# A whole-model kernel whose GpSimd makes part of the weights' low halves: another share for GpSimd, an earlier search, an earlier start of the gating

## Chip, cores and metric

The kernel runs on one core of a Trainium2 chip. The metric is the device time of one execution in microseconds (us), the lower the better. Engines are PE (TensorE, with PEld for its weight loads), DVE (VectorE), ACT (ScalarE), POOL (GpSimd) and SP (SyncE, which issues the DMAs of the weights).

## What is computed

Two transformer-like blocks on 256 tokens of 1024 features, all in float32. The first block is attention beside a gated recurrence, then PEER, a layer of 16384 experts of one neuron each, of which a token takes 16 for each of 8 heads. The second block is a convolution beside a linear recurrence (RG-LRU) with a gated linear layer behind it, and then a stick-breaking attention with another one. The change lies around PEER:

```python
def peer(x, wq, subkeys, u, v):                  # of one block of tokens xb
    qp = (xb @ wq).reshape(..., PEER_HEADS, 2, PEER_DKEY // 2)
    s = jnp.einsum('thcd,hcnd->thcn', qp, subkeys)      # 2 x 8 rows of 128 scores a token
    v1, i1 = lax.top_k(s[:, :, 0], 16)
    v2, i2 = lax.top_k(s[:, :, 1], 16)
    cand = v1[..., :, None] + v2[..., None, :]
    sc, p = lax.top_k(cand.reshape(..., 256), 16)       # eidx = (i1, i2) at p
    gates = jax.nn.softmax(sc, axis=-1)
    act = jax.nn.gelu(jnp.einsum('td,thkd->thk', xb, u[eidx]))
    return jnp.einsum('thk,thkd->td', gates * act, v[eidx])
```

## The kernel before

**Weights.** All weights stream through `load` in units of [128, 2048], two halves each. SyncE issues the DMA into `raw` (two buffers), ScalarE rounds a half to `hi` (L163), and `lo = raw - hi` (L168) is made by VectorE or by GpSimd; three buffers each of `hi` and `lo`, one unit ahead of use. A product takes three matmuls: x's high and low part by `hi`, and x's high part by `lo`. In `wstat` they make one chunk of 128 output columns with sixteen matmuls by `hi` (L196, L197) and then eight by `lo` (L199). So TensorE comes to a chunk's `lo` only after its sixteen matmuls by `hi`.

**Who makes `lo`.** `self.nsplit` counts the halves. GpSimd takes two of three halves of `pu` in its first 22 units and every other one behind them, and three of the first four halves of `wq`, `wi0`, `fgu0`, `wi1`, `fgu1`, the weights which follow a norm: 86 of 500 in all. VectorE makes the other 414.

**PEER.** Its stages are the query projection `wq` (16 chunks, each with two matmuls by `sk` that give the scores `s`, copied from PSUM for four columns at a time, L692), `pu` (128 chunks, every expert for all tokens, with GELU into `actA` and `actB`), and `pv` (the sum back over all experts). The gates of experts that a token doesn't take are zero. `topk` is the search of the sixteen best on VectorE. `best` takes two rounds of MAX8 and FIND_INDEX8 with one MATCH_REPLACE8 between (L719 to L722), over 128 scores or 64 sums. The sums `cand` (L735), the places, and the one-hots `oh` (L771 to L773) that look the places up follow. The search of the first 128 tokens (t = 0) and then that of the others are spread over the chunks of `pu` below `JT` = 56. From chunk 56 on `gate4` turns the places of four tokens into gates: one-hots A (L794) and B (L795) on VectorE, four matmuls of 128x128 (L797), products into the cells (L800, L803), and a copy by ScalarE of the chunks to come (L805). There are 64 of them, at chunks 56 to 123. `ga` (L818) is the product of the new chunk's GELU with the gates there already.

**Order.** The program is written in one sequence, and a scheduler gives each engine its own order; the queues run in order. The norms (`norm_t`) are chains of steps of one element a partition on VectorE (L291, L292 in `rsqrt1`); the first weights of the next product are split beside them. In `even`, ScalarE runs the tanh, exp and square root of the recurrence (L1024 to L1035) between the `hi` casts of `wi0`; the change of function costs an ACT_TABLE_LOAD.

Of the kernel before, what the change touches and what calls it, by code (L numbers as in the profile page):

```python
# [88 lines left out]
def layout(i):  # L89
# [11 lines left out]
    u = g("peer_u")[0].reshape(128, 64, 2, 8, 128)          # i1, unit, i2, k, p  # L101
# [32 lines left out]
# ---------------------------------------------------------------- the program  # L134
class Prog:
# [3 lines left out]
    # ---- streamed weights: units of [128, 2048], two halves each with hi and lo parts  # L139
    def stream_init(self):  # L140
# [7 lines left out]
        self.nsplit = 0  # L148

    LA = 1  # L150
    FIRST = ("wq", "wi0", "fgu0", "wi1", "fgu1")

    def load(self, n):
# [5 lines left out]
        for h in range(2):  # L159
# [21 lines left out]
    # ---- products  # L181
# [6 lines left out]
    def wstat(self, half, x, K=8):  # L188
        """W^T x for one chunk of 128 columns -> PSUM [128, 256]"""
# [12 lines left out]
    def xstat(self, acc, half, x, k, first, last, cg, ts=(0, 1)):  # L202
        """acc[t][c] += x_k^T W_k; x: hi, lo of [128, k, 256], or of [128, 128] for each t; cg: 512-column slices"""
# [16 lines left out]
    def out_n(self, nm, x, nk, step=None):  # L220
        """x^T W (K = nk*128, 1024 columns) -> acc[t][c] in PSUM; the first tokens are done first"""
# [17 lines left out]
    def out_n512(self, nm, j0, x, lead=0, step=None):  # L239
        """x^T W (K = 1024, 512 columns) -> acc[t] in PSUM; the first tokens lead by so many k"""  # L240
# [41 lines left out]
    def rsqrt1(self, pool, x):  # L282
        """x ** -0.5 for x [128, 1]"""
# [22 lines left out]
    def norm_t(self, pool, side, gain, shift=None, row=None):  # L306
        """rmsnorm(h) * gain (+ shift), hi and lo, features on partitions; gain, shift [128, 8];
        with a row, h is first replaced by rmsnorm(h) * row"""
# [89 lines left out]
    # ---- first block: MoBA attention and HGRN2  # L398
    def mix1(self):
# [20 lines left out]
        # f = lb + (1 - lb) (1 + tanh(x/2)) / 2  # L420
# [6 lines left out]
        # forget gates, queries  # L427
# [17 lines left out]
        for hd in range(4):  # L445
# [25 lines left out]
        # decayed products by halving: scT[b] holds s on partitions, (head, t) free  # L471
# [52 lines left out]
        def soft(c, qT, kT):  # L524
            """probabilities of heads 2c, 2c+1"""
# [26 lines left out]
                # (k0,q0) (k0,q1) (k1,q1)  # L552
# [13 lines left out]
        def decay(n=1):  # L566
            """n more levels begun, and those begun before done"""
# [74 lines left out]
    def add_res(self, t):  # L642
        """h += what the last stage left in PSUM, for tokens t"""
# [16 lines left out]
    # ---- PEER  # L660
    JT = 56

    def peer(self):
# [7 lines left out]
        with tc.tile_pool(name="pe", bufs=1) as p:  # L671
# [22 lines left out]
            for c in range(16):  # L694
                if c % 2 == 0:
                    u = self.unit("wq", c // 2)
                pt = self.wstat(u[c % 2], x)
                qps[c] = p3.tile([128, 256], F32, name="qp", bufs=3)
                nc.scalar.copy(qps[c], pt)
                if c:  # L700
                    scores(c - 1)
            scores(15)
            skp.__exit__(None, None, None)

            # the sixteen best of each half, of their sums, and their gates
            def topk(t):
                v = p2.tile([128, 16, 16], F32, name="v")
                iu = p2.tile([128, 16, 16], U32, name="iu")
                vi = p2.tile([128, 16, 16], F32, name="vi")
                gv = p2.tile([128, 8, 16], F32, name="gv")  # L710
                gp = p2.tile([128, 8, 16], U32, name="gp")
                ab = [p2.tile([128, 8, 16], F32, name=f"ab{n}") for n in range(2)]
                ai = p2.tile([128, 8, 16], U32, name="ai")
                res = [p2.tile([128, 8, 16], F32, name=f"res{n}") for n in range(3)]
                sm = p2.tile([128, 8], F32, name="gsm")

                def best(src, val, idx):
                    for r in range(2):
                        nc.vector.max(out=val[:, 8 * r:8 * r + 8], in_=src)  # L719
                        nc.vector.max_index(out=idx[:, 8 * r:8 * r + 8], in_max=val[:, 8 * r:8 * r + 8], in_values=src)  # L720
                        if r == 0:
                            nc.vector.match_replace(out=src, in_to_replace=val[:, 0:8], in_values=src, imm_value=-3.0e38)  # L722
# [21 lines left out]
                nc.vector.tensor_tensor(res[2], gv, gv[:, :, 0:1].to_broadcast([128, 8, 16]), op=ALU.subtract)  # L744
# [4 lines left out]
                # places in the halves: a = max(0, p / 8 - 1, p / 4 - 6, p - 48), and b = p less where row a begins,  # L749
                # min(16 a, 8 a + 8, 4 a + 24, a + 48)  # L750
# [471 lines left out]
```

## Time and profile before

| | |
|---|---|
| time, median of 3 runs | 1726.06 us (1725.60 to 1726.34) |
| span of the profiled execution | 1725.1 us |
| PE busy | 1606.9 us (93%) |
| DVE busy | 1320.7 us (77%) |
| ACT busy | 848.9 us (49%) |
| POOL busy | 251.2 us (15%), of which `lo` 213.7 us in 86 instructions |

The busy time of PE is an average over stages. The stages of PEER by the start of their first matmul: the query projection from 172.5 us, `pu`'s chunks 0 to 55 from 227.3, its chunks 56 to 127 from 415.5, `pv` from 706.2 to 1040. Columns of a timeline row: start, duration, engine, line, operation, output<-inputs, shape, count, and in brackets the idle time of the engine before it and what ended that. PE rows of a line are grouped where they follow each other (x8 is one chunk's eight matmuls by `lo`).

### The profile page before, as it was taken

To read this page: it belongs to the slowest core of one execution; us is meant where nothing else is said; L and a number is where in the kernel's file an instruction comes from. 1 tells how busy PE (TensorE), PEld (TensorE's weight loads), DVE (VectorE), ACT (ScalarE), POOL (GpSimd) and SP (SyncE) were. 2 spreads that over 40 slices of the span, in tenths; PEclk is the share of its full clock that TensorE was granted. 3 is DMA by queue.
4 is the path that set the end of the run, shared out by engine and by line. 5 is a ranking of instruction groups with operands and counts; after the bars stand their busy time and mean duration, and the time that the engine had idled before them with its cause. 6 is when DMAs were issued, how large, how long until landed. Compare 5 with 4: busy or idle time off the path is not lost.

```text
span 1725.1 us, 27616 instructions
## 1 busy us (share of the span) xinstructions
PE 1606.9 (93%) x10454; PEld 1461.7 (85%) x10454; DVE 1320.7 (77%) x2862; ACT 848.9 (49%) x1501; POOL 251.2 (15%) x113
## 2 busy tenths in 40 slices
PE   6997997899999998999999996997999799979998
PEld 6786997899999998888888885987998677769997
DVE  6967589834999999777787778877887778665544
ACT  6544452444433333555555554645444367754442
POOL 0302044443322233000000003001000100010000
PEclk9999998999999999999999998998999999989999
DMA  5424543364433343677777774564988643325554
GB/s 199 139 87 141 171 148 130 118 208 157 147 123 123 123 139 131 241 271 265 263 278 264 277 267 156 182 214 158 332 315 307 212 153 107 113 88 182 184 183 146
DMA packets 52405, 320.98 MB, mean 186 GB/s; under 512 B 5808, under 2 KB 6192, under 8 KB 20144
## 3 DMA queue, kind: packets, MB, share of 16 engines
q1 hardware_dynamic: 51264, 315.75, 52.6%
q10 hardware_dynamic: 1008, 3.47, 0.6%
q8 instruction: 82, 1.34, 0.3%
q14 instruction: 51, 0.42, 0.1%
HBM read 318.15 MB, written 1.05 MB: 185 GB/s over the span
## 4 chain that ended last, share of the span: by engine, by line
PE 70%; DVE 22%; issue 3%; ACT 3%; DMA 1%; POOL 0%; ACTq 0%; DVEq 0%; SPq 0%
PE acc L213 12%; PE acc L214 12%; PE acc L215 12%; PE pt L196 10%; PE pt L197 10%; PE pt L199 10%; DVE B L795 4%; DVE lo L168 3%; DVE A L794 3%; ACT hi L163 2%; DVE actA L800 1%; DVE oh L771 1%; PE pt L493 1%; DVE xn L302 1%; DVE actB L818 1%
## 5 line engine op out<-in xcount | busy, mean ns | idle before, releaser
L163 ACT CAST hi<-raw 128x1024 fp32r<-128x1024 f32 x500 | 524.2, 1051 | 483.7 <-PE pt L197 186.2
L168 DVE TENSOR_TENSOR lo<-raw,hi 128x1024 fp32r<-128x1024 f32 x414 | 513.4, 1241 | 294.9 <-ACT hi L163 289.7
L196 PE MATMUL pt<-xh,hi 128*128 128x256 f32 x2144 | 542.4, 290 | 11.9 <-ACT xh L357 11.2
L197 PE MATMUL pt<-xl,hi 128*128 128x256 f32 x2144 | 534.5, 286 | 0.4 <-DVE xl L358 0.4
L196 PEld LDWEIGHTS pt<-xh,hi 128*128 128x128 f32 x2144 | 417.8, 195 | 14.4 <-ACT xh L357 12.5
L197 PEld LDWEIGHTS pt<-xl,hi 128*128 128x128 f32 x2144 | 417.9, 195 | 0.9 <-DVE xl L358 0.7
L168 POOL TENSOR_TENSOR lo<-raw,hi 128x1024 fp32r<-128x1024 f32 x86 | 213.7, 2493 | 1137.9 <-ACT hi L163 858.4
L199 PE MATMUL pt<-xh,lo 128*128 128x256 f32 x2144 | 307.9, 287 | 17.2 <-DVE lo L168 17.2
L199 PEld LDWEIGHTS pt<-xh,lo 128*128 128x128 f32 x2144 | 282.2, 196 | 18.3 <-DVE lo L168 18.3
L214 PE MATMUL acc<-lo,wh 128*128 128x512 f32 x512 | 199.3, 389 | 0.7 <-DVE lo L168 0.7
L215 PE MATMUL acc<-hi,wl 128*128 128x512 f32 x512 | 199.3, 389 | 0.0
L213 PE MATMUL acc<-hi,wh 128*128 128x512 f32 x512 | 199.2, 389 | 0.0
L795 DVE TENSOR_SCALAR B<-iota,idxT,idxT 128x128 f32<-128x128 f32 x256 | 143.3, 560 | 0.0
L909 DVE SCALAR_TENSOR_TENSOR araw<-araw,sc 128x1024 f32<-128x1024 f32 x96 | 116.1, 1218 | 0.0
L214 PEld LDWEIGHTS acc<-lo,wh 128*128 128x128 f32 x512 | 96.1, 188 | 21.1 <-DVE lo L168 1.1
L215 PEld LDWEIGHTS acc<-hi,wl 128*128 128x128 f32 x512 | 96.1, 188 | 20.2 <-DVE wl L261 0.3
L213 PEld LDWEIGHTS acc<-hi,wh 128*128 128x128 f32 x512 | 96.1, 188 | 19.8
L805 ACT COPY actB<-acc 128x288 f32<-128x288 f32 (+31 forms) x64 | 18.4, 288 | 171.7 <-DVE actB L803 146.9
L797 PE MATMUL acc<-B,A 128*128 128x128 f32 x512 | 73.7, 280 | 17.7 <-DVE B L795 17.7
L794 DVE TENSOR_SCALAR A<-iota,idxT 128x128 f32<-128x128 f32 x256 | 88.4, 345 | 1.7 <-PE acc L797 1.7
L797 PEld LDWEIGHTS acc<-B,A 128*128 128x128 f32 x512 | 64.9, 192 | 21.9 <-DVE B L795 21.9
L214 PE MATMUL acc<-lo,yh 128*128 128x512 f32 x208 | 81.5, 392 | 0.0
(296 smaller groups left out, 1904.8 us busy)
## 6 DMA issues: line engine op xcount, KB each, us to landing
raw<-in_pu SPq DMA_DIRECT2D x64, 1024.0 KB, 4.9
raw<-in_pv SPq DMA_DIRECT2D x64, 1024.0 KB, 4.9
araw<-in_ada SPq DMA_DIRECT2D x96, 512.0 KB, 5.7
raw<-in_fgu SPq DMA_DIRECT2D x44, 1024.0 KB, 4.9
raw<-in_wi SPq DMA_DIRECT2D x22, 1024.0 KB, 4.9
raw<-in_fd SPq DMA_DIRECT2D x22, 1024.0 KB, 4.9
raw<-in_wp SPq DMA_DIRECT2D x14, 1024.0 KB, 5.0
raw<-in_wo SPq DMA_DIRECT2D x12, 1024.0 KB, 4.9
```

Of the source, the lines that this page charges most:

```text
L163: nc.scalar.copy(hi, s)
L168: ins = eng.tensor_tensor(lo, s, hi.bitcast(F32), op=ALU.subtract)
L196: nc.tensor.matmul(pt, hi[:, c], xh[:, k], start=k == 0, stop=False)
L197: nc.tensor.matmul(pt, hi[:, c], xl[:, k], start=False, stop=False)
L199: nc.tensor.matmul(pt, lo[:, k * 128:k * 128 + 128], xh[:, k], start=False, stop=k == K - 1)
L213: nc.tensor.matmul(a, xh, hi[:, cs], start=first, stop=False)
L214: nc.tensor.matmul(a, xh, lo[:, cs], start=False, stop=False)
L215: nc.tensor.matmul(a, xl, hi[:, cs], start=False, stop=last)
L794: nc.vector.tensor_scalar(A, iota, idxT[0][:, t:t + 1], None, op0=ALU.is_equal)
L795: nc.vector.tensor_scalar(B, iota, idxT[1][:, t:t + 1], idxT[2][:, t:t + 1], op0=ALU.is_equal, op1=ALU.mult)
L797: nc.tensor.matmul(gp[:, n], A, B, start=True, stop=True)
L909: nc.vector.scalar_tensor_tensor(w, w, 1.0, self.sc, op0=ALU.mult, op1=ALU.mult, accum_out=m[:, k:k + 1])
```

## The change

- GpSimd's share of `lo` is a table, `POOLED`: halves of `wq`'s units 2 to 7 and of `pu`'s units 0 to 5, so 24 halves, which are consecutive in the stream. VectorE makes the other 476. There is no GpSimd `lo` beside a norm or beside the gating.
- The search is cut in three. `halves` (the bests of the scores, both token halves in turn) starts at chunk 5 of the query projection; `sums` (the bests of the sums) and `places` come for t = 0 and t = 1 by a table of due chunks, `due`: fifteen steps in the chunks 0 to 11 of `pu`, fourteen in 12 to 33.
- `JT` is 40: the gating begins at chunk 40, and its 64 `gate4` lie in the chunks 40 to 123.
- Two small things of the second block go from GpSimd to VectorE: the scaling of `h` by the first norm (L361) and the two steps of `silu_c` in `even` (L883, L884).
- Comments are gone, so lines shift (L168 is L166 after; L719 to L722 are L700 to L703; A and B, L811 and L812; `ga`, L835; the recurrence of `even`, L1038 to L1049).

```diff
-    FIRST = ("wq", "wi0", "fgu0", "wi1", "fgu1")
+    POOLED = {"wq": (2, 8), "pu": (0, 6)}
...
-            self.nsplit += 1
-            eng = nc.vector
-            if (nm == "pu" and self.nsplit % (3 if j < self.JT // 2 - 6 else 2)) or (j < 2 and nm in self.FIRST and (j, h) != (1, 1)):
-                eng = nc.gpsimd
+            a, b = self.POOLED.get(nm, (0, 0))
+            eng = nc.gpsimd if a <= j < b else nc.vector
...
-                    nc.gpsimd.tensor_scalar(ht, ht, r1, None, op0=ALU.mult)
+                    nc.vector.tensor_scalar(ht, ht, r1, None, op0=ALU.mult)
...
-    JT = 56
+    JT = 40
...
+            def halves():
                 for c in range(16):
-                    best(s[t][:, c], v[:, c], iu[:, c])
-                    if c % 2 == 1:
-                        yield
+                    for t in range(2):
+                        best(s[t][:, c], v[t][:, c], iu[t][:, c])
+                    yield
+
+            def sums(t):
+                cand = p2.tile([128, 8, 64], F32, name="cand", bufs=2)
...
+                yield
                 for hd in range(8):
-                    best(cand[:, hd], gv[:, hd], gp[:, hd])
-                    yield
+                    best(cand[:, hd], gv[t][:, hd], gp[t][:, hd])
+                    if hd % 2:
+                        yield
+
+            def places(t):
...
+            hst = halves()
+            for c in range(16):
...
+                if c:
+                    scores(c - 1)
+                if c > 4:
+                    next(hst)
...
+            def steps():
+                yield from hst
+                for t in range(2):
+                    yield from sums(t)
+                for t in range(2):
+                    yield from places(t)
...
-            nst = 2 * (8 + 8 + 1 + 4 + 1)
-            k = 0
+            due = [i * 12 // 15 for i in range(15)] + [12 + i * 23 // 14 for i in range(14)]
+            n = 0
             for j in range(JT // 2):
                 u = self.unit("pu", j)
                 for h in range(2):
                     experts(2 * j + h, u[h])
-                while k < min(nst, (j + 1) * nst // (JT // 2 - 2) + 1):
-                    next(st, None)
-                    k += 1
+                    while n < len(due) and due[n] <= 2 * j + h:
+                        next(st, None)
+                        n += 1
...
-        self.silu_c(pa, self.sc, nc.gpsimd, 4)
+        self.silu_c(pa, self.sc, nc.vector, 4)
```

VectorE in the middle of the gating, before: the gates A and B of four tokens, the products (L800, L803, L818) and no `lo` in this chunk, which GpSimd makes.

```order
L818 TENSOR_TENSOR actB<-actB,ga 128x124
L800 TENSOR_TENSOR actA<-actA,acc 128x56x4
L803 TENSOR_TENSOR actB<-actB,acc 128x33x4
L794 TENSOR_SCALAR A<-iota,idxT_1689 128x128
L795 TENSOR_SCALAR B<-iota,idxT_1690,idxT_1691 128x128
L794 TENSOR_SCALAR A<-iota,idxT_1689 128x128
L795 TENSOR_SCALAR B<-iota,idxT_1690,idxT_1691 128x128
L794 TENSOR_SCALAR A<-iota,idxT_1689 128x128
L795 TENSOR_SCALAR B<-iota,idxT_1690,idxT_1691 128x128
L794 TENSOR_SCALAR A<-iota,idxT_1689 128x128
L795 TENSOR_SCALAR B<-iota,idxT_1690,idxT_1691 128x128
```

The same place after.

```order
L835 TENSOR_TENSOR actB<-actB,ga 128x124
L817 TENSOR_TENSOR actA<-actA,acc 128x40x4
L820 TENSOR_TENSOR actB<-actB,acc 128x41x4
L811 TENSOR_SCALAR A<-iota,idxT_1689 128x128
L812 TENSOR_SCALAR B<-iota,idxT_1690,idxT_1691 128x128
L811 TENSOR_SCALAR A<-iota,idxT_1689 128x128
L812 TENSOR_SCALAR B<-iota,idxT_1690,idxT_1691 128x128
L811 TENSOR_SCALAR A<-iota,idxT_1689 128x128
L812 TENSOR_SCALAR B<-iota,idxT_1690,idxT_1691 128x128
L811 TENSOR_SCALAR A<-iota,idxT_1689 128x128
L812 TENSOR_SCALAR B<-iota,idxT_1690,idxT_1691 128x128
L166 TENSOR_TENSOR lo<-raw,hi 128x1024
```

A chunk's `lo` now stands in VectorE's queue behind its four A and B, in every chunk.

VectorE where the one-hots of t = 0 are looked up, before (chunks 8 to 11 of `pu`).

```order
L168 TENSOR_TENSOR lo<-raw,hi 128x1024
L762 SCALAR_TENSOR_TENSOR ab_2333<-ab_2332,ab_2333 128x128
L771 TENSOR_TENSOR oh<-iota,ab_2332 128x1024
L763 TENSOR_TENSOR ab_2333<-gp,ab_2333 128x128
L772 TENSOR_TENSOR oh<-oh,vi 128x1024
L771 TENSOR_TENSOR oh<-iota,ab_2332 128x1024
L773 TENSOR_REDUCE res_2335<-oh 128x64
L772 TENSOR_TENSOR oh<-oh,vi 128x1024
L771 TENSOR_TENSOR oh<-iota,ab_2333 128x1024
L168 TENSOR_TENSOR lo<-raw,hi 128x1024
```

The same place after; the first L166 here is the first `lo` of `pu` on VectorE, that of chunk 12.

```order
L759 TENSOR_TENSOR ab_2933<-gp_1710,ab_2933 128x128
L768 TENSOR_TENSOR oh<-oh,vi 128x1024
L767 TENSOR_TENSOR oh<-iota,ab_2932 128x1024
L769 TENSOR_REDUCE res_2935<-oh 128x64
L768 TENSOR_TENSOR oh<-oh,vi 128x1024
L166 TENSOR_TENSOR lo<-raw,hi 128x1024
L769 TENSOR_REDUCE res_2935<-oh 128x64
L767 TENSOR_TENSOR oh<-iota,ab_2933 128x1024
L166 TENSOR_TENSOR lo<-raw,hi 128x1024
L768 TENSOR_TENSOR oh<-oh,vi 128x1024
L166 TENSOR_TENSOR lo<-raw,hi 128x1024
```

Ahead of that first `lo`, VectorE's queue has the bests of all scores and of all sums of both token halves, and the first steps of `places(0)`; before, it had those of t = 0 alone.

ScalarE in the recurrence of `even`, before: the cast of a half of `wi0` (L163) stands ahead of the change to the square root (L1035).

```order
L1029 ACTIVATE b<-r,c_79 128x256
L1028 ACTIVATE a<-r,n_80 128x256
L1015 COPY rxp<-pt 128x256
L1029 ACTIVATE b<-r,c_79 128x256
L163 CAST hi<-raw 128x1024
L1024 ACTIVATE r<-acc,hb 128x256
L1024 ACTIVATE ig<-acc,hb 128x256
L1035 ACT_TABLE_LOAD
L1035 ACTIVATE b<-b 128x256
L1024 ACT_TABLE_LOAD
```

The same place after.

```order
L1038 ACT_TABLE_LOAD
L1038 ACTIVATE r<-acc,hb 128x256
L1038 ACTIVATE ig<-acc,hb 128x256
L1049 ACT_TABLE_LOAD
L1049 ACTIVATE b<-b 128x256
L1042 ACT_TABLE_LOAD
L1042 ACTIVATE a<-r,n_80 128x256
L1043 ACTIVATE b<-r,c_79 128x256
L1049 ACT_TABLE_LOAD
L1049 ACTIVATE b<-b 128x256 x2
L163 CAST hi<-raw 128x1024 x2
```

Two table loads have come in, and the two casts come after all of them. (A number behind a name, as in ab_2332, tells buffers of one name apart.)

## Rows read from the trace of the kernel before

**Rows 1.** Windows, `pu`'s chunks 0-55, 56-127: length, busy PE, PEld, DVE, ACT, POOL; PEclk.

```profile
227.30:415.50 188.20, 170.96 (x1355) 169.94 (x1355) 130.49 (x389) 82.77 (x126) 87.15 (x35) 0.95 0.45 155
415.50:706.20 290.70, 272.98 (x2241) 268.77 (x2240) 279.74 (x739) 112.34 (x284) 84.48 (x35) 0.99 0.39 131
```

**Rows 2.** Timeline of PE: each chunk's matmuls by `lo`, in two places.

```profile
252.42 1.12 PE L199 MATMUL pt<-xh,lo 128*128 128x256 f32 x8
255.30 1.12 PE L199 MATMUL pt<-xh,lo 128*128 128x256 f32 x8
262.70 2.08 PE L199 MATMUL pt<-xh,lo 128*128 128x256 f32 x8 [4.36 <-DVE lo L168]
267.99 1.14 PE L199 MATMUL pt<-xh,lo 128*128 128x256 f32 x8
...
425.64 1.12 PE L199 MATMUL pt<-xh,lo 128*128 128x256 f32 x8
429.41 1.12 PE L199 MATMUL pt<-xh,lo 128*128 128x256 f32 x8
```

**Rows 3.** Timelines of POOL and DVE ahead of the wait at 262.70.

```profile
257.38 3.05 POOL L168 TENSOR_TENSOR lo<-raw,hi 128x1024 fp32r<-128x1024 f32 x1 [0.23 <-ACT hi L163]
...
258.16 3.36 DVE L771 TENSOR_TENSOR oh<-iota,ab 128x1024 f32<-128x1024 f32 x1
```

**Rows 4.** Busy time and granted clock (0.50) just behind that wait.

```profile
261.30:268.00 6.70, 5.30 (x25) 5.30 (x26) 6.70 (x7) 1.43 (x2) 0.00 (x0) 0.50 0.46 158
```

**Rows 5.** What PE waited for between 172 and 706 us.

```profile
PE acc L797 <- DVE B L795: 17.7, 22, 2.0
```

**Rows 6.** Timelines of POOL and DVE in the gating.

```profile
554.02 2.38 POOL L168 TENSOR_TENSOR lo<-raw,hi 128x1024 fp32r<-128x1024 f32 x1 [6.11 <-DVE B L795]
...
554.09 2.40 DVE L795 TENSOR_SCALAR B<-iota,idxT,idxT 128x128 f32<-128x128 f32 x1
...
559.19 1.23 DVE L168 TENSOR_TENSOR lo<-raw,hi 128x1024 fp32r<-128x1024 f32 x1 [0.19 <-ACT hi L163]
560.34 0.29 DVE L818 TENSOR_TENSOR actB<-actB,ga 128x132 f32<-128x132 f32 x1
...
561.05 0.28 DVE L794 TENSOR_SCALAR A<-iota,idxT 128x128 f32<-128x128 f32 x1
...
561.50 0.28 DVE L794 TENSOR_SCALAR A<-iota,idxT 128x128 f32<-128x128 f32 x1
```

**Rows 7.** Timelines of POOL and DVE at two bests of 128 scores.

```profile
220.13 2.40 POOL L168 TENSOR_TENSOR lo<-raw,hi 128x1024 fp32r<-128x1024 f32 x1 [53.21 <-ACT hi L163]
...
220.21 0.47 DVE L719 MAX8 v<-s 128x8 f32<-128x128 f32 x2
...
222.34 0.28 DVE L720 FIND_INDEX8 iu<-v,s 128x8 uint32<-128x128 f32 x1
```

**Rows 8.** DVE at two bests of 64 sums, from one to the next.

```profile
237.01 0.34 DVE L719 MAX8 gv<-cand 128x8 f32<-128x64 f32 x2
...
238.71 0.34 DVE L719 MAX8 gv<-cand 128x8 f32<-128x64 f32 x2
```

**Rows 9.** Copies of scores; adds of sums: duration min/median/max (ns), first and last start.

```profile
L692 ACT COPY s<-acc x8: 586/597/607, 190.4 to 228.0; 128x512 f32<-128x512 f32 x8
...
L735 DVE TENSOR_TENSOR cand<-v x8: 212/313/2219, 232.9 to 295.7; 128x128 f32<-128x128 f32 x4, 128x192 f32<-128x192 f32 x2, 128x64 f32<-128x64 f32 x2
```

**Rows 10.** POOL and DVE in the norm ahead of the first gated layer.

```profile
1165.57 7.98 POOL L168 TENSOR_TENSOR lo<-raw,hi 128x1024 fp32r<-128x1024 f32 x3 [85.69 <-ACT hi L163]
...
1168.47 2.29 DVE L291 SCALAR_TENSOR_TENSOR r<-r,rm 128x1 f32<-128x1 f32 x1
```

**Rows 11.** ACT and PE in the recurrence of `even`.

```profile
1089.92 0.47 ACT L1024 ACTIVATE r<-acc,hb 128x256 f32<-128x256 f32 x1 [0.42 <-PE acc L1023]
...
1102.26 1.28 ACT L1035 ACT_TABLE_LOAD   x1
...
1105.57 0.39 PE L196 MATMUL pt<-xh,hi 128*128 128x256 f32 x1 [0.75 <-ACT hi L163]
```

More of the change, by code (lines that the diff above doesn't have):

```diff
@@ L692, in scores @@
                         nc.scalar.copy(s[t][:, c - 3:c + 1], sp[t])
[L694 to L722, printed above, removed]
-                for c in range(16):
-                    best(s[t][:, c], v[:, c], iu[:, c])
-                    if c % 2 == 1:
-                        yield
-                nc.vector.tensor_copy(vi, iu)
-                cand = p2.tile([128, 8, 64], F32, name="cand")
-                vv = v.rearrange("p (h two) k -> p h two k", two=2)
@@ new lines, in peer, with best @@
+            v = [p2.tile([128, 16, 16], F32, name=f"v{t}") for t in range(2)]
+            iu = [p2.tile([128, 16, 16], U32, name=f"iu{t}") for t in range(2)]
+            gv = [p2.tile([128, 8, 16], F32, name=f"gv{t}") for t in range(2)]
+            gp = [p2.tile([128, 8, 16], U32, name=f"gp{t}") for t in range(2)]
+            def best(src, val, idx):
+                for r in range(2):
+                    nc.vector.max(out=val[:, 8 * r:8 * r + 8], in_=src)
+                    nc.vector.max_index(out=idx[:, 8 * r:8 * r + 8], in_max=val[:, 8 * r:8 * r + 8], in_values=src)
+                    if r == 0:
+                        nc.vector.match_replace(out=src, in_to_replace=val[:, 0:8], in_values=src, imm_value=-3.0e38)
@@ L733, in topk @@
+            def halves():
+                for c in range(16):
+                    for t in range(2):
[3 more added lines that the diff above has]
+                cand = p2.tile([128, 8, 64], F32, name="cand", bufs=2)
+                vv = v[t].rearrange("p (h two) k -> p h two k", two=2)
                 o = 0
@@ L739, in topk @@
                     o += na * nb
+                yield
                 for hd in range(8):
-                    best(cand[:, hd], gv[:, hd], gp[:, hd])
-                    yield
-                nc.vector.tensor_tensor(res[2], gv, gv[:, :, 0:1].to_broadcast([128, 8, 16]), op=ALU.subtract)
+                    best(cand[:, hd], gv[t][:, hd], gp[t][:, hd])
+                    if hd % 2:
+                        yield
+            def places(t):
+                vi = p2.tile([128, 16, 16], F32, name="vi")
+                ab = [p2.tile([128, 8, 16], F32, name=f"ab{n}") for n in range(2)]
+                ai = p2.tile([128, 8, 16], U32, name="ai")
+                res = [p2.tile([128, 8, 16], F32, name=f"res{n}") for n in range(3)]
+                sm = p2.tile([128, 8], F32, name="gsm")
+                nc.vector.tensor_copy(vi, iu[t])
+                nc.vector.tensor_tensor(res[2], gv[t], gv[t][:, :, 0:1].to_broadcast([128, 8, 16]), op=ALU.subtract)
                 nc.scalar.activation(res[2], res[2], AF.Exp)
@@ L748, in topk @@
                 nc.vector.tensor_tensor(res[2], res[2], sm[:, :, None].to_broadcast([128, 8, 16]), op=ALU.mult)
+                yield
                 aa, bb = ab
-                nc.vector.tensor_scalar(ai, gp, 3, None, op0=ALU.logical_shift_right)
+                g = gp[t]
+                nc.vector.tensor_scalar(ai, g, 3, None, op0=ALU.logical_shift_right)
                 nc.vector.tensor_scalar(aa, ai, -1.0, 0.0, op0=ALU.add, op1=ALU.max)
-                nc.vector.tensor_scalar(ai, gp, 2, None, op0=ALU.logical_shift_right)
+                nc.vector.tensor_scalar(ai, g, 2, None, op0=ALU.logical_shift_right)
                 nc.vector.scalar_tensor_tensor(aa, ai, -6.0, aa, op0=ALU.add, op1=ALU.max)
-                nc.vector.scalar_tensor_tensor(aa, gp, -48.0, aa, op0=ALU.add, op1=ALU.max)
+                nc.vector.scalar_tensor_tensor(aa, g, -48.0, aa, op0=ALU.add, op1=ALU.max)
                 st = p2.tile([128, 8, 16], F32, name="st")
@@ L779, in topk @@
                 yield
+            hst = halves()
+            for c in range(16):
+                if c % 2 == 0:
+                    u = self.unit("wq", c // 2)
+                pt = self.wstat(u[c % 2], x)
+                qps[c] = p3.tile([128, 256], F32, name="qp", bufs=3)
+                nc.scalar.copy(qps[c], pt)
+                if c:
+                    scores(c - 1)
+                if c > 4:
+                    next(hst)
+            scores(15)
+            skp.__exit__(None, None, None)
+            def steps():
[4 more added lines that the diff above has]
+                    yield from places(t)
             done = [0]
@@ L818, in experts @@
                     nc.vector.tensor_tensor(lo, lo, tmp[:, 0:g], op=ALU.mult)
-            def steps():
-                yield from topk(0)
-                yield from topk(1)
             st = steps()
-            nst = 2 * (8 + 8 + 1 + 4 + 1)
-            k = 0
+            due = [i * 12 // 15 for i in range(15)] + [12 + i * 23 // 14 for i in range(14)]
+            n = 0
             for j in range(JT // 2):
```

3 lines of the change are left out of this document (1 added, 2 removed).

## The prediction

> **What bounds the kernel now.** I read the page's busy shares first: PE is busy 93% of the span, so a change of VectorE and GpSimd can win only PE's gaps. Then the windows by stage [rows 1], PE's timeline for its pace [rows 2], PE's waits [rows 5], and the timelines of VectorE and GpSimd at such waits.
>
> Pace: a chunk of `pu` takes 255.30 - 252.42 = 2.88 us on PE, and 429.41 - 425.64 = 3.77 us with a `gate4`, which so costs 0.89 [rows 2]. Chunks 0 to 55 need 56 x 2.88 = 161.3 us and took 188.2; chunks 56 to 127 need 72 x 2.88 + 64 x 0.89 = 264.3 and took 290.7 [rows 1]. These stages lose 26.9 and 26.4 us.
>
> To what: VectorE's `oh` from 258.16, 1.1 us of work elsewhere, took 3.36, and ended with GpSimd's `lo`, which had begun at 257.38 and took 3.05 [rows 3]. The next in VectorE's queue was a `lo`, and PE waited 4.36 us for it; the chunk took 7.40 us instead of 2.88, and the one behind it 5.29 [rows 2], at a granted clock of 0.50, the 1.2 GHz level [rows 4]. So a stop costs its length and about 2.4 us more. In the gating, B from 554.09 took 2.40 us, for as long as GpSimd's `lo` from 554.02 [rows 6]; PE waited for B 22 times, 17.7 us in all [rows 5]. I call this the lock: while GpSimd makes a `lo`, such steps of VectorE stand until it ends.
>
> **The gating without GpSimd.** The change takes every GpSimd `lo` out of the gating and hands it to VectorE. From row to row a `lo` costs VectorE 560.34 - 559.19 = 1.15 us, the three products 561.05 - 560.34 = 0.71, an A and its B 561.50 - 561.05 = 0.45 [rows 6]. A chunk with a `gate4` is 1.15 + 0.71 + 4 x 0.45 = 3.66 us of VectorE against PE's 3.77; one without is 1.15 + 0.2 = 1.35 against 2.88. The gating now has 88 chunks with the same 64 `gate4`, so 24 chunks give back 1.5 us each. VectorE keeps pace, if narrowly. The `lo` waits behind the four B in its queue (the order shown), and what waits for it is a later chunk. In the trace VectorE's `lo` at 559.19 follows four B with no stop of PE. I take all 26.4 us as won: **-26.4**. Bounds: 0 here would mean that VectorE paces the gating, a rival below.
>
> **The search beside GpSimd.** GpSimd's 24 `lo` run beside MAX8, FIND_INDEX8 and MATCH_REPLACE8. Do those stand too? Two bests of 128 scores ran from 220.21 to about 222.54, 1.17 us each, with GpSimd's `lo` over the whole of it, 220.13 to 222.53, and the last FIND_INDEX8 took 0.28 [rows 7]. They don't stand. The pages speak for something else here: the Trainium skill, "SBUF — State Buffer", Who interferes with whom, says that a VectorE instruction with two SBUF inputs contends with a GpSimd instruction that reads SBUF; FIND_INDEX8 and MATCH_REPLACE8 take two by their operands. By that rule the search would stand and the sum would be that of the third rival; the row speaks against it.
>
> So the old stops in chunks 0 to 55 go, apart from 0.9 that I leave: **-26.0**.
>
> **A new stop at chunk 12.** VectorE's first `lo` in `pu`, that of chunk 12, is queued behind all of `halves`, both `sums` and the first `places` (the order shown). When does VectorE come to it? The scores are copied in four groups of columns, the last one at 228.0 to 228.6 [rows 9]; eight bests of 1.17 bring that to 238. Sixteen bests of 64 sums are 1.70 for two [rows 8], 13.6, and the eight adds of `cand` 0.2 to 0.3 each [rows 9], in all 253.5. The steps of `places(0)` ahead of the `lo`, five of the one-hot kind at 1.1 and a dozen small ones at 0.2, bring 261.5, and the `lo` is there at about 262.7. PE asks for it at 227.3 + 12 x 2.88 + 1.9 (sixteen matmuls by `hi`, two thirds of 2.88) = 263.8. Unlocked it is an us early. But the adds of `cand` can lock: one of eight stood 2.2 us in the trace [rows 9], and now GpSimd makes twelve halves of `pu` there at 2.4 us, 29 of 34.6 us. If four of eight stand 2.0 us each, the `lo` is 7 us late. Behind it the clock falls for a chunk: 6.6 + 2.4 = **+9**. With none standing it is 0, with six 14. Behind it are in VectorE's queue the rest of the lookups and the next `lo`; each chunk then has 2.88 us of PE for one `lo` of 1.15 and 1.7 us of search, and the search ends near chunk 30, ten chunks ahead of the gating. SyncE's queue waits only for `raw`, which a `lo` on VectorE (1.15 us instead of 2.4) frees no later.
>
> **The norms.** Three `lo` on GpSimd, 7.98 us, run beside the norm ahead of the first gated layer, and a step of one element, L291, took 2.29 us there [rows 10], about ten times what it takes beside no `lo`; of its kind three stood there, 1.5 to 2.3 us each, some 5.4 us lost in all. After, VectorE makes these three itself, 3 x 1.15 = 3.45, between the steps. Net -2.0, for four norms (`even`, both gated layers, `odd`): **-8**. Bounds: -15 if half of the 3.45 hides in VectorE's own waits, -3 if only one or two norms gain. The scaling of `h` and `silu_c` move four instructions of 1024 columns to VectorE, at most 1.15 us each, the price of a `lo`: 4.6 us. No step of the first chunks' products asks for them, so 0; without that cover 4.6.
>
> **ScalarE in `even`.** The scheduler has also turned the recurrence's steps: two table loads more, and the casts of halves 6 and 7 of `wi0` behind all of them (the order shown). Before, from the tanh at 1089.92 to the chunk that begins with half 7 at 1105.57 [rows 11] lay four loads and the cast of half 6. That chunk's cast began about 1104.5, 14.6 us after the tanh. After, the same stretch has six loads and no cast: 14.6 - 0.9 + 2 x 1.28 [rows 11] = 16.2, so the cast of half 6 begins at 1106.1 and ends at 1107.1. PE would be free for it at 1105.57 - 0.75 - 2.88 = 1101.9. It waits 5.2, and the clock falls behind it, 2.4: **+8**. Bounds: 0 if the steps wait less than the order lets one think, +12 if the waits for VectorE's steps between the loads grow. A table load shows 1.28 us here, with its next instruction 1.29 behind it; the Trainium skill, "ScalarE: Activation LUTs", What ACT_TABLE_LOAD costs, adds a drain of 1.38 us to each. By that the two new loads would be 2.8 us dearer and the time 1686.
>
> **Sum.** -26.4 - 26.0 + 9 - 8 + 8 = -43.4. On the span of the profiled execution, 1725.1, that is 1681.7; the median of the runs is 1.0 above that span, so **1683 us**.
>
> **Rivals.** *No new stop*: the adds don't lock and the casts come in time. The +9 and +8 fall away: 1666. For it: one add stood long in the trace, and ScalarE's order has no wait of its own. Against: the 24 `lo` of GpSimd come nearly without a pause.
>
> *Hand-off in the gating*: VectorE has 3.66 of 3.77 us, and PE's gate matmuls, VectorE's products and the next gates wait for each other in a ring. If half of the 64 chunks lose 0.5 us there, that is +16: 1699. For it: a spare of 0.11 us is small. Against: the stops of the trace begin with GpSimd's `lo`.
>
> *The search stands*: 24 `lo` at 2.4 us put 58 us of standing into VectorE's search, some 46 of it ahead of chunk 12, and PE stops there for 46 + 2.4 instead of 9: 1722. Against: [rows 7].
>
> *VectorE paces the gating, slower than before*: what PE waits for at B is then not the lock but the `lo` ahead in VectorE's queue, and giving it 38 `lo` more makes every gate chunk like the slow ones. A slow chunk loses 17.7 us / 22 = 0.80 of waiting [rows 5], with the slower clock behind it say 1.04; at each of 64 it is 66 us, against the 43.4 won: 1749. It decides from 43.4 / 64 = 0.68 us a chunk. Against: VectorE's sum is below PE's pace, and 2.40 us for one B begins with GpSimd's `lo` [rows 6].
>
> *It doesn't do what it says*: the order shows 24 `lo` on GpSimd in one run and none elsewhere, so no chance.
>
> **How the numbers follow.** Forecast 0.62, no new stop 0.13, hand-off 0.14, the search stands 0.04, VectorE paces 0.07. About 0.2%, 3.5 us, is what a measurement of this kernel can tell from no change. Forecast, no new stop and hand-off are faster: 0.89. 1722 is at that bound, so its 0.04 is same; slower 0.07. The range takes in the two neighbours, 1666 and 1699, and from the unknown costs their middle: 1664 to 1705. That leaves out the last two rivals and the ends of the forecast's own bounds, which all together would reach 1658 to 1708.
>
> **What would show it.** In the profile after: POOL with 24 `lo` between 180 and 260 us and none later; no A or B above 0.4 us; the windows of chunks 0 to 39 near 115 us plus the stop, of 40 to 127 near 310; one stop of some 6 us for VectorE's `lo` near 264; the L291 steps of the later norms at a tenth of 2.29; a PE wait for ScalarE's `hi` near chunk 6 of `wi0`. Wrong would be a wait for B or `lo` in every gate chunk, FIND_INDEX8 of over 2 us, or stops that recur after chunk 14.

## The result and the profile after

The changed kernel takes 1680.68 us (median; 1679.69 to 1681.72), the kernel before beside it 1725.83 (1724.67 to 1726.34). The ratio is 0.9737, 95% interval 0.9723 to 0.9751, so 45 us are won. The forecast was 1683, in a range of 1664 to 1705.

The page of the changed kernel, its first lines: busy time, share of the span, instructions.

```profile
span 1677.9 us, 27543 instructions
## 1 busy us (share of the span) xinstructions
PE 1591.5 (95%) x10454; PEld 1450.6 (86%) x10454; DVE 1274.2 (76%) x2944; ACT 867.9 (52%) x1519; POOL 84.9 (5%) x47
```

VectorE is busy for less time than before (1320.7), although it makes 62 `lo` more: time in which it stood counted as busy. In its profile the changed kernel is 47.2 us shorter than the one before; the runs' medians say 45.2 (the profiled execution was the fastest of the changed kernel's four, 1679.69 us).

The windows of `pu` after, columns as in [rows 1]: its chunks 0 to 39, and its chunks 40 to 127 with the gating.

```profile
227.20:354.30 127.10, 120.41 (x976) 119.85 (x976) 106.78 (x306) 61.44 (x96) 24.11 (x10) 0.97 0.49 168
354.30:664.50 310.20, 310.20 (x2625) 310.19 (x2625) 268.56 (x806) 150.03 (x333) 0.00 (x0) 1.00 0.43 150
```

The gating fills PE to the last tenth of a microsecond: 88 x 2.88 + 64 x 0.89 = 310.4 us is its pace, 310.2 its time, at a granted clock of 1.00. Chunks 0 to 39 need 115.2 and take 127.1. The longest waits of PE from the query projection to the end of `pu` (us in total, times, longest):

```profile
PE pt L338 <- DVE xn L334: 7.3, 1, 7.3
PE pt L197 <- DVE lo L166: 3.6, 1, 3.6
PE pt L194 <- ACT hi L163: 3.1, 1, 3.1
```

The 7.3 us belong to the norm ahead of the projection (before had such a wait too). The other two make most of the 11.9 us: with the slower clock behind them, chunk 10 is 4.7 us over its pace and chunks 12 and 13 are 5.4; chunk 0 has 1.1, which it had before too. The 22 waits for B [rows 5] are gone. So are the five for VectorE's `lo` in the old chunks 0 to 55:

```profile
PE pt L199 <- DVE lo L168: 17.2, 5, 4.4
```

For a `lo` of GpSimd itself PE had no wait there. Two waits are new, one for `lo` at chunk 12 and one for ScalarE's `hi`. A VectorE chunk of the gating after, from `lo` to `lo`:

```profile
500.00 1.23 DVE L166 TENSOR_TENSOR lo<-raw,hi 128x1024 fp32r<-128x1024 f32 x1 [1.46 <-ACT hi L163]
501.14 0.28 DVE L835 TENSOR_TENSOR actB<-actB,ga 128x124 f32<-128x124 f32 x1
...
503.36 0.34 DVE L812 TENSOR_SCALAR B<-iota,idxT,idxT 128x128 f32<-128x128 f32 x1
503.76 1.23 DVE L166 TENSOR_TENSOR lo<-raw,hi 128x1024 fp32r<-128x1024 f32 x1
```

It is 503.76 - 500.00 = 3.76 us, PE's pace, and the last B takes 0.34 where [rows 6] has 2.40.

By stages the profiled executions differ so, read from the ends of the chunks' last matmuls in both traces (after minus before): norm and projection +1.1, `pu` -42.4, the norm of `even` -4.3, the recurrence of `even` +7.8, the norms of the first gated layer, `odd` and the second gated layer -3.8, -0.9 and -3.4. The rest, -1.3, lies in small shifts and in the kernel's beginning.

### The profile page after: what moved, and what is told of

Read it like the earlier page. It is cut to its first block, busy times and chain, and to the rows that moved or that the text cites. A ratio compares the mean times of both kernels' runs of the same rounds, so it can differ in the third digit from the quotient of the medians.

```text
span 1677.9 us, 27543 instructions
## 1 busy us (share of the span) xinstructions
PE 1591.5 (95%) x10454; PEld 1450.6 (86%) x10454; DVE 1274.2 (76%) x2944; ACT 867.9 (52%) x1519; POOL 84.9 (5%) x47
## 4 chain that ended last, share of the span: by engine, by line
PE 88%; DVE 8%; ACT 2%; issue 1%; DMA 1%; POOL 0%; DVEq 0%; ACTq 0%
PE pt L194 15%; PE pt L195 14%; PE pt L197 14%; PE acc L212 12%; PE acc L211 12%; PE acc L213 12%; PE acc L814 3%; DVE lo L166 2%; PE pt L491 1%; PE pt L1136 1%; ACT hi L163 0%; DVE xn L300 0%; DMA cr<-in_rows 0%; PE acc L688 0%; DVE cand L719 0%
## 5 line engine op out<-in xcount | busy, mean ns | idle before, releaser
L166 DVE TENSOR_TENSOR lo<-raw,hi 128x1024 fp32r<-128x1024 f32 x476 | 582.0, 1225 | 275.9 <-ACT hi L163 265.0
L163 ACT CAST hi<-raw 128x1024 fp32r<-128x1024 f32 x500 | 524.4, 1050 | 489.9 <-PE pt L195 231.6
L197 PE MATMUL pt<-xh,lo 128*128 128x256 f32 x2144 | 302.7, 284 | 3.6 <-DVE lo L166 3.6
L197 PEld LDWEIGHTS pt<-xh,lo 128*128 128x128 f32 x2144 | 278.0, 193 | 3.9 <-DVE lo L166 3.8
L812 DVE TENSOR_SCALAR B<-iota,idxT,idxT 128x128 f32<-128x128 f32 x256 | 86.9, 339 | 0.0
L213 PE MATMUL acc<-hi,yl 128*128 128x512 f32 x208 | 81.1, 390 | 0.0
L211 PE MATMUL acc<-hi,yh 128*128 128x512 f32 x208 | 80.8, 391 | 0.0
L258 ACT CAST wh<-actB 128x128 fp32r<-128x128 f32 x176 | 48.9, 297 | 58.0 <-PE acc L212 53.9
L338 PE MATMUL pt<-ident,xn 128*128 128x128 f32 x96 | 22.0, 412 | 53.0 <-DVE xn L334 52.5
L822 ACT COPY actB<-acc 128x352 f32<-128x352 f32 (+31 forms) x64 | 20.2, 315 | 100.5 <-DVE actB L820 97.1
```

Source lines behind the costliest of these rows:

```text
L163: nc.scalar.copy(hi, s)
L166: ins = eng.tensor_tensor(lo, s, hi.bitcast(F32), op=ALU.subtract)
L197: nc.tensor.matmul(pt, lo[:, k * 128:k * 128 + 128], xh[:, k], start=False, stop=k == K - 1)
L211: nc.tensor.matmul(a, xh, hi[:, cs], start=first, stop=False)
L213: nc.tensor.matmul(a, xl, hi[:, cs], start=False, stop=last)
L258: self.nc.scalar.copy(hi, src)
```

## Experiments

Two theories stood against each other. **The lock**: VectorE's steps stand while GpSimd makes a `lo`, so what wins is that GpSimd's `lo` are gone. **The order**: what wins is the earlier search and the earlier, longer gating, with GpSimd's help where it fits. The kernel before is run beside each.

### The gating's `lo` alone

```diff
-            if (nm == "pu" and self.nsplit % (3 if j < self.JT // 2 - 6 else 2)) or ...
+            if (nm == "pu" and j < self.JT // 2 and self.nsplit % (3 if j < self.JT // 2 - 6 else 2)) or ...
```

> The kernel before, with VectorE alone making the low parts of pu from chunk 56 on; search, JT = 56 and norms as before. If GpSimd's lock made the gating's stops: chunks 56 to 127 take 264 us instead of 290.7, no B above 0.4 us, the time 1725.8 - 26 = 1700 (1696 to 1704). If VectorE paces the gating: slower than before, up to 1770. If the earlier start at chunk 40 is what won the gating's time: 1726.

1700.51 us against 1726.43, ratio 0.985 (0.9834 to 0.9867): 26 us. The window of chunks 56 to 127 in this kernel, to be read beside the second line of [rows 1]:

```profile
415.80:679.90 264.10, 264.10 (x2241) 264.09 (x2240) 247.75 (x774) 124.76 (x285) 0.00 (x0) 1.00 0.43 144
```

264.1 us, the pace that the prediction worked out, 264.3, and 26.6 less than before. The same gates and the same number of `lo` lie in the same 72 chunks; only who makes the `lo` has changed. VectorE doesn't pace the gating, and its start need not move. That B stood for GpSimd's `lo` shows in the trace of the kernel before too: the 34 B that ran beside one took 2.40 us (median), the other 222 took 0.34.

### The gating from chunk 56 in the changed kernel

```diff
-    JT = 40
+    JT = 56
```

> The changed kernel with the gating again from chunk 56 (64 gates in 68 chunks instead of 84); the dates of the search are unchanged. If the lock is all, VectorE still keeps pace with 3.66 of 3.77 us a chunk: the time of the changed kernel, 1681 (1678 to 1684). If the spare of 0.11 us is not enough where gate chunks follow each other without a pause: 10 to 16 us slower, 1691 to 1697.

1679.60 us (1678.70 to 1680.75), the changed kernel's time. `pv` begins 0.8 us later than in the changed kernel's trace, and a delay of 0.9 is there already at the start of `pu`. So `JT` = 40 gave nothing, and 3.66 us of VectorE in 3.77 of PE are enough even with 64 gates in 68 chunks: the hand-off rival falls.

### All `lo` of `pu` on VectorE in the kernel before

```diff
-            if (nm == "pu" and self.nsplit % ...) or (j < 2 and nm in self.FIRST and (j, h) != (1, 1)):
+            if (j < 2 and nm in self.FIRST and (j, h) != (1, 1)):
```

> The kernel before with every low part of pu on VectorE; the search stays behind the projection and token half by token half, the norms' low parts stay on GpSimd. If the lock alone made the stops of chunks 0 to 55 too: 1726.4 - 26.4 - 25 = 1675 (1671 to 1680). If these stops need the earlier and rearranged search, or GpSimd's help beside it: only the gating's gain, 1700, or above, with waits for VectorE's lo in chunks 0 to 55.

1680.55 us against 1726.16, ratio 0.9732 (0.9716 to 0.9748). This is the changed kernel's time, with the old search in its old place and the norms as they were. Chunks 0 to 55 and 56 to 127 of it:

```profile
227.00:396.40 169.40, 165.71 (x1354) 164.81 (x1353) 139.69 (x424) 82.66 (x126) 0.00 (x0) 0.98 0.52 173
396.40:660.50 264.10, 264.10 (x2241) 264.10 (x2241) 247.61 (x774) 124.74 (x284) 0.00 (x0) 1.00 0.43 144
```

188.2 us have become 169.4, of which nearly 7, in chunks 29 to 31, are a stop of another kind (below). The time is 5.5 us above the expected 1675, just outside the stated 1671 to 1680, and that stop is more than this. The order's theory falls for `pu` as a whole: neither the three-part search nor its early start is needed.

That the two times are equal is a balance of unlike parts. Read stage by stage, the changed kernel is ahead of this one by some 11 us in the norms, and behind it by 7.8 in the recurrence of `even`, 2.8 in `pu` and 1.2 in the projection.

### No `lo` on GpSimd in the changed kernel

```diff
-    POOLED = {"wq": (2, 8), "pu": (0, 6)}
+    POOLED = {}
```

> The changed kernel with all 500 low parts on VectorE, none on GpSimd. If GpSimd's help beside the search is needed: 24 times 1.15 us = 27.6 us more in VectorE's queue by chunk 12, of which the 12 in the query projection fall into VectorE's waits for scores; some 5 us slower, 1686 (1681 to 1697). If the lock on the sums and places costs as much as GpSimd gives: 1681 or below.

1675.99 us (1673.62 to 1677.86), ratio 0.9707 (0.9691 to 0.9723): some 5 us better than the changed kernel, where 5 worse was expected if the help is needed. The two intervals of the ratio touch; in the profiles `pv` begins 4.0 us earlier than in the changed kernel, 0.9 of it there at the start of `pu`. PE's longest waits in the projection and `pu`:

```profile
PE pt L197 <- DVE lo L166: 2.8, 3, 2.0
PE pt L194 <- ACT xh L355: 1.6, 1, 1.6
PE acc L773 <- DVE res L769: 1.0, 1, 1.0
```

No wait for `hi`, and three for `lo`, of 2.0 us at most. The 24 `lo` that GpSimd still made beside the search cost more than they gave: 4.7 us by these medians, 2.9 where the same edit is made in the kernel with the casts ahead (below).

### The exp on ScalarE, and the copies of the scores

What is the new wait for `hi`? ScalarE, PE and VectorE of the changed kernel around it:

```profile
248.94 1.28 ACT L739 ACT_TABLE_LOAD   x1
258.87 0.31 ACT L739 ACTIVATE res<-res 128x128 f32<-128x128 f32 x1 [8.64 <-DVE res L738]
259.08 1.03 ACT L163 CAST hi<-raw 128x1024 fp32r<-128x1024 f32 x1
...
260.16 0.58 PE L194 MATMUL pt<-xh,hi 128*128 128x256 f32 x1 [3.06 <-ACT hi L163]
...
271.88 1.22 DVE L166 TENSOR_TENSOR lo<-raw,hi 128x1024 fp32r<-128x1024 f32 x1
...
273.15 1.67 PE L197 MATMUL pt<-xh,lo 128*128 128x256 f32 x8 [3.63 <-DVE lo L166]
```

The softmax's exp (L739, in `places`) waits 8.6 us in ScalarE's queue for a VectorE step (L738) that stands behind the whole of `sums`. Behind it in ScalarE's queue is a cast of `hi`, and PE waits for that at chunk 10. It then waits for VectorE's first `lo` at chunk 12. The test holds the exp until the latest cast:

```diff
-            nc.scalar.copy(hi, s)
+            self.last_hi = nc.scalar.copy(hi, s)
...
-                nc.scalar.activation(res[2], res[2], AF.Exp)
+                with tc.issue_after(self.last_hi.ins):
+                    nc.scalar.activation(res[2], res[2], AF.Exp)
```

> The changed kernel with the softmax's exp of the search held on ScalarE until the latest cast of hi. If the stop at chunk 10 comes from that exp, which waits on ScalarE for VectorE with a cast behind it: that stop, 4.7 us with its clock, goes; GpSimd's last two low parts come earlier, and chunk 12 waits about as long as now: 1676 (1674 to 1678). If VectorE was late anyhow and the waiting only moves to chunk 12: 1681.

1677.22 us (1674.89 to 1678.87); `pu` is 3.8 us shorter in the profile, counted from the projection's end. The stop at chunk 10 is gone, and chunk 12 waits longer:

```profile
269.76 2.08 PE L197 MATMUL pt<-xh,lo 128*128 128x256 f32 x8 [4.58 <-DVE lo L166]
```

Here the stop of the prediction can be seen by itself. VectorE in the same kernel, ahead of that `lo`:

```profile
238.17 1.99 DVE L719 TENSOR_TENSOR cand<-v 128x128 f32<-128x128 f32 x1
...
240.82 2.55 DVE L719 TENSOR_TENSOR cand<-v 128x128 f32<-128x128 f32 x3
...
250.07 2.00 DVE L719 TENSOR_TENSOR cand<-v 128x192 f32<-128x192 f32 x3
...
268.49 1.22 DVE L166 TENSOR_TENSOR lo<-raw,hi 128x1024 fp32r<-128x1024 f32 x1
```

Three of eight adds stood, by about 1.7, 1.9 and 1.4 us beyond 0.3 for one and 0.6 for three. That is 5.0 us, and PE waited 4.6: by this sum the `lo` would have come just in time without the lock on the adds. It is a sum and not a run.

The kernel before with all of `pu` on VectorE has a stop behind the exp too. Its chunk 30 takes 7.63 us; PE waits 2.0 of them for `hi`, behind the exp of the second token half:

```profile
314.26 0.31 ACT L745 ACTIVATE res<-res 128x128 f32<-128x128 f32 x1 [4.60 <-DVE res L744]
```

With the exp held there (a kernel below) chunk 30 takes 3.05 us. Now the changed kernel with the scores copied for two columns at a time (and the exp held):

```diff
-                    if c % 4 == 3:
-                        nc.scalar.copy(s[t][:, c - 3:c + 1], sp[t])
+                    if c % 2 == 1:
+                        nc.scalar.copy(s[t][:, c - 1:c + 1], sp[t])
```

> As the kernel with the exp held, and the scores copied for two columns at a time instead of four, so the search starts on the last columns sooner. If VectorE's late arrival at the low part of chunk 12 is set by the wait for the last four columns: VectorE comes 4 to 5 us sooner, three more steps of the lookup at 1.13 us stand ahead of it, so 1 to 2 us better than with the exp alone, 1674.5 (1673 to 1676). If it is set by the lock on sums and places: as with the exp alone, within 1 us.

1676.19 us (1675.23 to 1677.68), 1 us from the one with the exp alone, and PE waits 4.8 us at chunk 12. The intervals overlap, so the run doesn't tell the two apart, and it doesn't show what part of the stop is the wait for the last columns. Its trace shows something else. VectorE comes to the adds earlier, none of them stands long, and three later steps stand in their place, one of 1.36 us and these two, which take 0.2 to 0.3 us where they don't stand:

```profile
250.33 2.48 DVE L751 TENSOR_SCALAR ai<-gp 128x128 uint32<-128x128 uint32 x1
...
253.16 2.48 DVE L753 SCALAR_TENSOR_TENSOR ab<-gp,ab 128x128 f32<-128x128 uint32 x1
```

Together they lose some 5.5 us, about as much as the adds did. Which steps of the search GpSimd's `lo` hit changed with the timing; in both kernels some were hit.

### The norms

```diff
-    FIRST = ("wq", "wi0", "fgu0", "wi1", "fgu1")
+    FIRST = ()
```

in the kernel before.

> The kernel before, with the first four halves behind each norm on VectorE; the rest as before, ScalarE's order in the recurrence as before too. If the three low parts of GpSimd beside a norm lock its one-element steps: the sum over the norms in the changed kernel's trace, -11, so 1715 (1711 to 1719). If the changed kernel's gain in the norms came from the scaling of h and silu_c on VectorE: 1724 to 1726.

1714.25 us against 1726.43, ratio 0.9933 (0.9916 to 0.995): 12 us. The stages moved by -3.8 (`even`), -3.8, -1.2 and -3.3 in its profile, much as in the changed kernel, with the scaling of `h` and `silu_c` still on GpSimd. So the `lo` are the cause. The norm of [rows 10] in the changed kernel:

```profile
1126.25 2.36 DVE L166 TENSOR_TENSOR lo<-raw,hi 128x1024 fp32r<-128x1024 f32 x2 [0.16 <-ACT hi L163]
1128.53 0.21 DVE L289 SCALAR_TENSOR_TENSOR r<-r,rm 128x1 f32<-128x1 f32 x1
...
1129.33 1.22 DVE L166 TENSOR_TENSOR lo<-raw,hi 128x1024 fp32r<-128x1024 f32 x1
1130.46 0.21 DVE L289 SCALAR_TENSOR_TENSOR r<-r,rm 128x1 f32<-128x1 f32 x1
```

Three `lo` of 1.14 us each between steps of 0.21, where one step took 2.29.

### The casts of `wi0`

In the changed kernel ScalarE casts halves 6 and 7 behind the recurrence, and PE waits for them:

```profile
1043.90 0.47 ACT L1038 ACTIVATE r<-acc,hb 128x256 f32<-128x256 f32 x1 [1.14 <-PE acc L1037]
...
1058.74 1.28 ACT L1049 ACT_TABLE_LOAD   x1
1060.03 0.72 ACT L1049 ACTIVATE b<-b 128x256 f32<-128x256 f32 x2
1060.66 1.98 ACT L163 CAST hi<-raw 128x1024 fp32r<-128x1024 f32 x2
...
1061.74 0.58 PE L194 MATMUL pt<-xh,hi 128*128 128x256 f32 x1 [6.86 <-ACT hi L163]
```

One line ahead of the exp and tanh puts the loading of that unit, and so its casts, ahead in the program:

```diff
+        un[2] = self.unit("wi0", 2)
         for c in range(4):
             nc.scalar.activation(a[:, c], r[:, c], AF.Exp, scale=n8[:, c:c + 1])
```

> The changed kernel with unit 3 of wi0 loaded ahead of the recurrence's exp and tanh in the program, which puts the casts of its halves ahead on ScalarE (16 table loads in all, not 20). If the casts behind the table loads make the stop at chunk 6 of wi0: the wait of 6.9 us and its slow clock go, 1672 (1671 to 1674). If the projection then waits for the recurrence's own steps: 1679 to 1681.

1671.86 us (1670.96 to 1673.79), ratio 0.9685 (0.9668 to 0.9701), 8.8 better than the changed kernel. In its profile chunk 6 of `wi0` ends 9.1 us earlier, and PE has no wait for `hi` there. The line changes a second thing: from the first exp of the recurrence to its last square root there are two table loads instead of six. PE's wait doesn't hang on that, for the two casts stand ahead of the second load already. ScalarE of this kernel:

```profile
1047.31 1.06 ACT L163 CAST hi<-raw 128x1024 fp32r<-128x1024 f32 x1
1049.99 1.05 ACT L163 CAST hi<-raw 128x1024 fp32r<-128x1024 f32 x1 [0.49 <-PE pt L195]
1054.45 1.28 ACT L1050 ACT_TABLE_LOAD   x1
```

### Put together

The changed kernel with `POOLED = {}` and the casts ahead:

> The changed kernel with all low parts on VectorE and the casts of wi0 ahead of the recurrence. If the two gains lie in different stages and add: 1676 - 8.8 = 1667 (1665 to 1669). If they don't add: near 1672.

1668.91 us (1667.02 to 1669.89). The two gains add within 2 us. With the exp held as well:

> As the one before, and the search's exp held until the latest cast. Without GpSimd PE waited for no cast at the exp, so if the remaining stops are VectorE's low parts behind the search: as the one before, within 2 us. If the exp's table loads still delayed casts: 2 to 4 us better.

1665.84 us (1665.14 to 1668.07), 3 us better, as the second theory gave. But the runs of the two kernels overlap, and of the 4.0 us between their profiles `pu` has only 1.4, so the time alone doesn't decide. The trace speaks for the exp's place: PE's chunk 15 fell from 5.14 us in the kernel without GpSimd to 3.40, and the wait of 2.0 us there is gone.

The kernel before with no `lo` on GpSimd (the two edits for `pu` and for the norms together) and the exp held, search and `JT` as they were:

> The kernel before with all low parts on VectorE and the search's exp held; search, JT = 56, scaling of h and silu_c as before. If no part of the moved search is needed: 1680.5 - 12 for the norms - 2 to 5 for the stop at chunk 30 that the exp makes: 1665 (1662 to 1668), the changed kernel beaten by 15. If the moved search earns its place: above 1675.

1664.49 us (1663.96 to 1667.89), ratio 0.9643 (0.963 to 0.9656): 16 us below the changed kernel. Its waits of PE from the projection to the end of `pu`:

```profile
PE pt L196 <- ACT xh L357: 1.6, 1, 1.6
PE pt L199 <- DVE lo L168: 1.2, 2, 0.7
PE acc L214 <- DVE lo L168: 0.2, 1, 0.2
```

And the changed kernel with no `lo` on GpSimd, casts ahead, exp held, and the search spread out again:

```diff
-            due = [i * 12 // 15 for i in range(15)] + [12 + i * 23 // 14 for i in range(14)]
+            due = [i * 24 // 15 for i in range(15)] + [24 + i * 28 // 14 for i in range(14)]
...
-    JT = 40
+    JT = 56
```

> The changed kernel with all low parts on VectorE, casts ahead, exp held, the search's dates spread over 52 chunks and the gating from chunk 56. The stops left in chunks 8 to 22 without GpSimd were 7 us in all. If they come from the search's density: most go, 1662 (1660 to 1665). If from what the scheduler puts ahead of a low part whatever the dates: 1667.

1662.47 us (1661.80 to 1662.83), ratio 0.9626 (0.9613 to 0.964), the best of this study: 18 us below the changed kernel, 64 below the one before. It is 3.4 below the same kernel with the dense search, 2.6 of it in `pu`: without GpSimd's `lo` the crowding of the search into 34 chunks costs some 3 us (`JT` alone gave nothing above). PE's waits for `lo` in the projection and `pu` are four of 0.3 us at most.

```profile
PE pt L194 <- ACT xh L355: 1.6, 1, 1.6
PE pt L197 <- DVE lo L166: 1.1, 4, 0.3
```

## Why the prediction was right, and where it wasn't

- **The gating, -26.4**: right. 310.2 us after, worked out 310.4; doing this part alone gave 26 us.
- **The old stops of chunks 0 to 55, -26.0**: right in size and cause. `pu` lost 26.9 + 26.4 us before and loses 11.9 - 0.2 after, and the old search without GpSimd's `lo` in `pu` keeps only 8 of the first 26.9 (169.4 against 161.3).
- **The new stop at chunk 12, +9**: wrong in its shape, and the sum is near by luck. `pu` beyond its pace is 11.7 us against 0.9 + 9. But there are two stops, 4.7 us at chunk 10 and 5.4 at chunks 12 and 13. That at chunk 10 (7.62 us for a chunk of 2.88) comes from ScalarE's queue, where the exp of the softmax waits with a cast behind it. This step the prediction didn't have: it followed VectorE's queue, and not the one that the exp stands in. The stop at chunk 12 is a `lo` behind the search, as described, but smaller: 3.6 us of waiting (4.6 with the exp held), where 6.6 was assumed. Three adds stood, where four were assumed, and two steps behind them which the prediction didn't count; they take 0.22 and 1.22 us where they don't stand:

```profile
260.33 2.40 DVE L756 TENSOR_SCALAR st<-ab 128x128 f32<-128x128 f32 x1
...
262.86 3.45 DVE L767 TENSOR_TENSOR oh<-iota,ab 128x1024 f32<-128x1024 f32 x1
```

  Beside them ran GpSimd's last two `lo`, from 260.2 and 262.8 us, whose casts had been queued behind the exp. With the exp held these two `lo` began at 252.3 and 254.9, and neither step stood.
- **The slower clock behind a stop, 2.4 each**: too much in the changed kernel. Chunk 10 took 7.62 - 2.88 - 3.06 = 1.7 us beyond its wait, chunks 12 and 13 together 7.22 + 3.92 - 2 x 2.88 - 3.63 = 1.8, chunk 6 of `wi0` 11.67 - 2.88 - 6.86 = 1.9. The stop of [rows 2], counted over both its chunks in the same way, is 7.40 + 5.29 - 2 x 2.88 - 4.36 = 2.6.
- **The norms, -8**: right in kind, mis-sized. They gave 4.3 + 3.8 + 0.9 + 3.4 = 12.4, and 12.1 by themselves in the kernel before. The three `lo` on VectorE were priced at their full 3.45 us a norm. At the norm of [rows 10] the three steps had lost some 5.4 us and the stage gained 3.8, so by this sum about half of the 3.45 lies in times in which VectorE waits. The 12.4 is nearer to the bound that was named, 15, than to the 8. It is also the miss: the forecast of the profiled span, 1681.7, is 3.8 us above the measured 1677.9, and the norms are 4.4 of that; the other terms nearly cancel.
- **ScalarE in `even`, +8**: right. The wait was 6.9 us instead of 5.2, the clock behind it 1.9 instead of 2.4; the stage lost 7.8, and taking the casts ahead gave 8.8. A table load is 1.28 us here too, and the next instruction begins 1.29 us after it began; no drain of 1.38 us stands behind it, and with two such drains the stage would have lost 10.6. So the trace differs from the Trainium skill, "ScalarE: Activation LUTs", What ACT_TABLE_LOAD costs, at this place.
- **The rivals.** *The search stands*: in the changed kernel 64 FIND_INDEX8 ran from 192 to 240 us, 56 of them beside a `lo` of GpSimd in whole or in part:

```profile
L701 DVE MATCH_VALUE_LOAD iu<-v,s x64: 67/73/94, 192.1 to 240.1; 128x8 f32 x64
L701 DVE FIND_INDEX8 iu<-v,s x64: 279/284/291, 192.1 to 240.2; 128x8 uint32<-128x128 f32 x64
```

None took over 0.291 us (columns: min, median and max in ns, first and last start). The prediction counted two inputs by the operands in the program. The rows show two instructions: a MATCH_VALUE_LOAD with the 128x8 values stands ahead of each FIND_INDEX8, whose own input is 128x128. So these rows don't speak against the rule on two SBUF inputs (the Trainium skill, "SBUF — State Buffer", Who interferes with whom); the prediction drew a rival from it that it doesn't give. For the two-input adds and one-hots the trace agrees with the rule: 1.7 to 2.2 us for an add and 3.45 for a one-hot beside a `lo`, 0.2 to 0.3 and 1.22 without. *VectorE paces the gating* and *hand-off* fell with the first two experiments, *no new stop* by the trace.
- **Slips that change nothing in the sum.** The `oh` of [rows 3] didn't end with GpSimd's `lo`, at 260.43, but at 261.52: it stood until the `lo` ended and then took its own 1.1 us, which is the lock all the same. Of the eight adds before, two stood and not one, 1.62 and 2.22 us. In the gating of the kernel before, GpSimd made 35 `lo` [rows 1] and not 38. The bounds as they are named reach 1701 at the upper end and not 1708.

What the prediction did not ask was whether the rest of the change is needed. It isn't: of its parts, the search's move, `JT` = 40 and GpSimd's 24 `lo` give nothing that the runs show, and the 24 `lo` cost some 3 to 5 us.

## What to carry to other kernels

A second engine's help is worth what it takes off the first one less what the first one stands for it: a `lo` on GpSimd saved VectorE 1.15 us and could stand it for 2.4, and with 0.11 us a chunk to spare VectorE still did better alone. When a change moves a chain, follow each step into the queue of the engine that runs it, and ask what is behind it there: an exp of 0.31 us stopped PE because a cast was queued behind it. When a change with several parts pays, run each part alone; here one line gave the changed kernel's whole time, because what the other parts won in the norms they lost again elsewhere. With the norms' `lo` on VectorE too and one or two repairs of ScalarE's order, the kernels were 16 to 18 us faster still.

## What the runs showed of the hardware that was not expected

The clock came back sooner than taken. Behind the wait of 3.06 us at chunk 10 the granted clock was 0.50, the 1.2 GHz level, for 3.2 us of PE's work, and then 1.00. Behind the wait of 6.86 us ahead of chunk 6 of `wi0` it was 0.50 for 3.8 us.

```profile
260.20:263.40 3.20, 3.20 (x15) 3.20 (x16) 3.20 (x5) 3.19 (x5) 3.04 (x2) 0.50 0.02 5
263.50:267.60 4.10, 4.10 (x37) 4.10 (x36) 4.10 (x8) 1.97 (x4) 1.73 (x1) 1.00 0.32 82
...
1061.74:1065.50 3.76, 3.76 (x17) 3.76 (x18) 3.76 (x5) 2.39 (x4) 0.00 (x0) 0.50 0.00 0
```

In [rows 4] PE worked 5.30 us at 0.50. At half of the clock half of such a time is lost: 1.6, 1.9 and 2.65 us, near the 1.7, 1.9 and 2.6 counted above. So a stop's price beyond its length is half of the time that PE then works at 0.50. It doesn't grow with the stop here: the wait of 6.86 us cost less than that of 4.36 in [rows 2]. What sets the time no run here shows.
